# Four more buffers of weight halves between two MLPs, a lead of six units, and sums kept in PSUM

## The chip, the cores and the metric

The kernel runs on one core of a Trainium2 chip. The metric is the device time of one execution in microseconds (us), and a kernel's time is the median of its runs. An engine takes its instructions in the order of the program: TensorE (PE) multiplies, VectorE (DVE) and ScalarE (ACT) work elementwise, GpSimd (POOL) too, and SyncE (SP) issues most of the DMAs. They wait for one another by semaphores. "raw", "wh", "acc" and so on are names of buffers in the program.

## The reference, cut to what matters

Two blocks on 256 tokens of width 1024, all in fp32. The first has two layers, each a mixer and an MLP; the second is an attention block on the result and a context. The change touches the end of the first MLP, the second mixer and the second MLP:

```python
def rmsnorm(x, g):
    xf = x.astype(jnp.float32)
    y = xf * lax.rsqrt(jnp.mean(xf * xf, axis=-1, keepdims=True) + EPS)
    return (y * g.astype(jnp.float32)).astype(x.dtype)

def mixer_c(h, w_in, conv_w, conv_b, w_r, b_r, w_i, b_i, lam, w_out):
    u = h @ w_in
    gate, xr = jnp.split(u, 2, axis=-1)
    xr = causal_depthwise_conv(xr, conv_w) + conv_b
    y = rg_lru(xr, w_r, b_r, w_i, b_i, lam) * jax.nn.gelu(gate)
    return y @ w_out

def sq_relu_mlp(h, w_up, w_down):
    return jnp.square(jax.nn.relu(h @ w_up)) @ w_down

def first_block(...):
    for layer in range(DEPTH):        # DEPTH = 2
        h = rmsnorm(x, mix_norm[layer])
        y = mixer_ab(...) if layer % 2 == 0 else mixer_c(...)
        x = x + y
        x = x + sq_relu_mlp(rmsnorm(x, mlp_norm[layer]), w_up[layer], w_down[layer])
    return rmsnorm(x, final_norm)

def second_block(x, c, ctx, ...):
    shift, scale, gate = jnp.split((silu(c) @ w_mod + b_mod)[:, None, :], 3, axis=-1)
    ...
    hc = rmsnorm_2(ctx, norm_g) * (1 + scale_c) + shift_c
    ...
```

`rg_lru` makes two gates r and i from block matrices of 128 x 128, and runs the recurrence h_t = a_t h_(t-1) + b_t over the tokens.

## The kernel before, in words

Activations lie transposed, 128 features on the partitions and 256 tokens along a row, eight such tiles for the width. All large weights come as 240 units of 128 x 1024 values (512 KB), in the order in which they are used. `fetch` (L277) issues a unit's DMA on SP into one of four `raw` buffers. `prep` (L298) splits it: `wh` is the unit rounded to the matmul's format, made on ACT (L301) or DVE (L303), and `wl` what is left, made by a subtraction on DVE or POOL (L304). `POLICY` (L40) names the engines for each sort of unit, and "ag" is ACT then GpSimd, "vg" DVE then GpSimd, "av" ACT then DVE. Halves go into a ring of six slots each. `mm3` (L347) multiplies a 128 x 128 piece in three matmuls, wh·xh, wh·xl and wl·xh (L349 to L351), where xh and xl are the same two halves of the activations. A unit is 24 such matmuls of 256 columns.

`unit` (L330) hands the next unit to a matmul, and first calls `ready` until two more units than the one needed are prepared (`self.ahead`). It also runs one entry of a background list (`tick`): during MLP 0 these are the products of the second block's modulation, 40 `mdump` on DVE (L868) of 12 weight tiles `mw` of 1 MB. A scheduler then places the instructions of all engines by their order in the program and their dependencies; no order is written out by hand.

Stages: layer 0, MLP 0, layer 1, MLP 1, and the second block beginning with `b2_head`. An MLP (`mlp`, L924) takes sixteen pairs of "up" units and, two pairs later, two "down" units each, that add into four PSUM banks `acc`. Its end is `proj_tail` (L803): for each of four pairs of rows b, the last matmuls, the product `mtmp` of the bank with the row scale R2 (L820), the addition to x (L821), the scaled split `xsh`, `xsl` (L826, L832), and the square `sqt` (L840), which DVE adds to the running sums `s` (L842). POOL adds the two halves of `s` (L846).

Layer 1 (`layer1`, L968) multiplies its "xr" units by the unnormalised halves, has PE sum `s` over the partitions (L413), makes the rsqrt `rc` on POOL (L424) and spreads it by PE (L431) to R; the results are scaled by R (L1014) and go through the convolution (L1022), the gates of eight heads (`xch`, `xcl`, then L998 to L1007), the "cg" units (L1028, L1030), the scan (L1044), the split into `ysh` and `ysl` (both in a slot whose first part bears the name `xr`), and the "wo1" units. In the unit order: six xr, ri0, two xr, ri1, eight cg, eight wo1.

`b2_head` (L1083) multiplies the context's halves `hch`, `hcl` by four units into two PSUM banks `c0` and `c1`, and between them sums `s` and makes R for the second block. PSUM has eight banks, four under the tag "acc" and four under "mm", each handed out in turn.

Of the kernel before, what the change touches and what calls it, by code (L numbers as in the profile page):

```python
# [12 lines left out]
F32R = mybir.dt.float32r  # L13
AF = mybir.ActivationFunctionType
ALU = mybir.AluOpType
AX = mybir.AxisListType

T = 256
# [4 lines left out]
NEG = -1e30  # L23
CHUNK = 1
RING = 6
RAW = 4
NT = 4
MT = 28
# [216 lines left out]
class Kern:  # L245
    def __init__(self, tc, aps, names, ctx):
        self.tc, self.nc, self.a, self.names, self.ctx = tc, tc.nc, aps, names, ctx
        self.n = 0
        self.u = 0
        self.raw = None  # L250
        self.bg = []
        self.q = []
        self.cnt = {}
        self.ahead = 2

    def pool(self, name, space=None):
        return self.tc.tile_pool(name=name, bufs=1) if space is None else \
# [48 lines left out]
    def ready(self):  # L306

        i = self.u
        name = self.names[i]
        r = self.fetch(name)  # L310
        wh = self.t(self.wp, [128, 1024], "wh", F32R, bufs=RING)
        wl = self.t(self.wp, [128, 1024], "wl", F32R, bufs=RING)
        if i == 0:
            for q in range(4):
                for k in (2 * q, 2 * q + 1):
                    self.split_scaled(self.x[:, k], self.p("mix", k), self.xs[0][:, k], self.xs[1][:, k])
                if q % 2 == 0:
                    c = slice(q * 256, q * 256 + 512)
                    self.prep(r[:, c], wh[:, c], wl[:, c], "a", "v")
        elif i == 1:  # L320
            for c in (slice(0, 512), slice(512, 1024)):
                self.prep(r[:, c], wh[:, c], wl[:, c], "a", "v")
        else:
            c = POLICY.get(name, ("av",))
            c = c[self.cnt.get(name, 0) % len(c)]
            self.prep(r, wh, wl, c[0], c[1])
        self.cnt[name] = self.cnt.get(name, 0) + 1
        self.q.append((name, (wh, wl)))
# [117 lines left out]
    def run(self):  # L446
        nc, ctx = self.nc, self.ctx
        V, S, G, PE = nc.vector, nc.scalar, nc.gpsimd, nc.tensor
        self.wp = ctx.enter_context(self.pool("wp"))
        self.pad(self.wp, 384)  # L450
        self.cp = ctx.enter_context(self.pool("cp"))
        self.dp = ctx.enter_context(self.pool("dp", bass.MemoryType.DRAM))
        self.psum = ctx.enter_context(self.pool("psp", bass.MemoryType.PSUM))
        cp = self.cp
        warm = self.warm = self.t(cp, [128, 1], "warm")
        G.memset(warm, 0.0)
        S.activation(warm, warm, AF.Tanh)
        self.par = self.t(cp, [128, NPAR], "par")
        nc.sync.dma_start(self.par, self.a["par"])
        with self.pool("xp") as xp:  # L460
            self.x = self.t(xp, [128, 8, T], "x")
            self.s1 = self.t(xp, [128, 2, T], "s1")
            self.s2 = self.t(xp, [128, 2, T], "s2")
            self.ident = self.t(cp, [128, 128], "ident")
            make_identity(nc, self.ident)
            self.ones = self.t(cp, [128, 128], "ones")
            G.memset(self.ones, 1.0)
            self.mhalf = self.t(cp, [128, 4], "mhalf")
            G.memset(self.mhalf, -0.5)
            self.pad(cp, 32)  # L470
            with self.pool("l0") as lp:
                self.pad(lp, 128)
                self.layer0(lp)
            with self.pool("m0") as mp:
                self.pad(mp, 128)
                self.mod_setup(mp)
                self.mlp(mp, 0)
                self.flush()
                self.mod_finish()
            with self.pool("l1") as lp:  # L480
                self.pad(lp, 128)
                self.layer1(lp)
            with self.pool("m1") as mp:
                self.pad(mp, 128)
                self.hc = self.new_h("hc")
                self.ctx_setup(mp)
                self.mlp(mp, 1)
                self.flush()
            with self.pool("b2h") as hp:
                st = self.b2_head(hp)  # L490
        with self.pool("b2") as bp:
            self.pad(bp, 128)
            with self.pool("b2e") as ep:
                self.b2_kv(bp, ep, st)
            with self.pool("b2a") as ap:
                self.b2_attn(bp, ap, st)
            with self.pool("b2o") as op:
                self.b2_out(op, st)
        assert self.u == N_UNITS
# [303 lines left out]
    def proj_tail(self, acc, name, ins, gname, g0, xs, R2=None, mp=None, sums=(), after=None):  # L803

        nc = self.nc
        V, S, G = nc.vector, nc.scalar, nc.gpsimd
        x = self.x
        with self.tc.issue_after(after.ins) if after else nullcontext():
            ws = [self.unit(name) for _ in ins]
        n = len(ins)  # L810
        late = []
        for b in range(4):
            for i in range(n):
                self.krow(acc, ws[i], ins[i], False, i == n - 1, (2 * b, 2 * b + 1))
            xb = x[:, 2 * b:2 * b + 2]
            if R2 is None:
                V.tensor_tensor(xb, xb, self.pair(acc[b]), op=ALU.add)
            else:
                tmp = self.t(mp, [128, 2, T], "mtmp", bufs=2)
                V.tensor_tensor(tmp, self.pair(acc[b]), self.b2(R2), op=ALU.mult)  # L820
                V.tensor_tensor(xb, xb, tmp, op=ALU.add)  # L821
            ks = (2 * b, 2 * b + 1)
            g = [self.p(gname, g0 + k) for k in ks]
            if xs is not None:
                for k in ks:
                    S.activation(xs[0][:, k], x[:, k], AF.Copy, scale=g[k % 2])  # L826
            for f in late:
                f()
            late = []
            if xs is not None:  # L830
                for k in ks:
                    V.scalar_tensor_tensor(xs[1][:, k], x[:, k], g[k % 2], xs[0][:, k].bitcast(F32),  # L832
                                           op0=ALU.mult, op1=ALU.subtract)
            for i, (st, scaled) in enumerate(sums):
                q = st if b == 0 else self.t(mp, [128, 2, T], f"sqt{i}", bufs=2)
                if scaled:
                    for k in ks:
                        S.activation(q[:, k % 2], x[:, k], AF.Square, scale=self.p(scaled, k))
                else:
                    S.activation(q, xb, AF.Square)  # L840
                if b:
                    late.append(lambda st=st, q=q: V.tensor_tensor(st, st, q, op=ALU.add))  # L842
        for f in late:
            f()
        for st, _ in sums:
            G.tensor_tensor(st[:, 0], st[:, 0], st[:, 1], op=ALU.add)  # L846
# [77 lines left out]
    def mlp(self, mp, l):  # L924
        nc = self.nc
        V, S, G, PE = nc.vector, nc.scalar, nc.gpsimd, nc.tensor
        x, xs = self.x, self.xs
        acc = [self.ps("acc") for _ in range(4)]
        A = {}
        R2 = None  # L930
# [3 lines left out]
        def up(p):  # L934
            ps = first[p] if p < 2 else self.gpair(("up", "up"), xs)
            r = self.t(mp, [128, 512], "mr", bufs=2)
            a = self.t(mp, [128, 512], "ma", bufs=2)
            ah = self.t(mp, [128, 512], "mah", F32R, bufs=4)
            al = self.t(mp, [128, 512], "mal", F32R, bufs=4)
            S.activation(r, ps, AF.Relu)  # L940
            S.activation(ah, r, AF.Square)
            G.tensor_tensor(a, r, r, op=ALU.mult)  # L942
            self.lo(al, a, ah)
            A[2 * p] = (ah[:, :T], al[:, :T])
            A[2 * p + 1] = (ah[:, T:], al[:, T:])

        for p in range(16):
            up(p)
            if p == 4:
                parts = self.ssq(mp, x)  # L950
            if p == 6:
                v = self.meaneps(self.csum(parts), D)
                rv = self.t(self.cp, [128, 2], "rv")
                V.reciprocal(rv, v)
            if p == 8:
                R2 = self.spread(mp, rv, "R2")
            if p >= 2:
                for k in (2 * p - 4, 2 * p - 3):
                    self.krow(acc, self.unit("down"), A.pop(k), k == 0, False)
# [8 lines left out]
    def layer1(self, lp):  # L968
# [12 lines left out]
        gl = self.t(lp, [128, 8, T], "gl")  # L981
        parts = [self.s1[:, 0]]
        rc = []
        pss = self.gfirst("xr", xs, lambda: rc.append(self.rsq(self.meaneps(self.csum(parts), D))))
        R = self.spread(lp, rc[0], "R")

# [527 lines left out]
```

## Time and profile before

| | |
|---|---|
| Median of three runs | 834.56 us (834.39 to 838.01) |
| Profiled execution, device time | 835.34 us |
| Its span | 833.5 us |
| Mean granted clock of PE in it | 0.986 |
| PE busy | 792.4 us (95%) |
| DVE busy | 593.0 us (71%) |
| ACT busy | 457.9 us (55%) |
| POOL busy | 224.8 us (27%) |
| MLP 0 | about 115 to 298 us |
| Layer 1 | about 298 to 398 us |
| MLP 1 | about 398 to 573 us |

A row of a timeline gives start and duration in us, then engine, line and operation, what it writes and reads, how many it stands for, and in brackets how long the engine was idle before it and what ended that. The chain that ended last is 68% PE, 12% DVE and 7% DMA. Starts of matmuls of 256 columns follow one another by 0.113 us where PE is fed.

### The profile page before, as it was taken

The numbers are of one execution on the slowest core, as the hardware profiler recorded it, in microseconds if no ns is written. First come the engines' busy times: TensorE is split into PE (matmuls) and PEld (weight loads), VectorE is DVE, ScalarE is ACT, GpSimd is POOL, SyncE is SP. The second block draws the span as 40 slices with busy tenths as digits, with TensorE's granted clock in tenths as the row PEclk, the third lists the DMA queues.
The fourth block names the chain that finished last, engine by engine and source line by source line (L and its number), as shares of the span: only waits on it lengthen the run. The fifth ranks groups of instructions, "written<-read, shape, count | busy, mean of one in ns | idle before, by whom it ended". The sixth has DMA issues, their size and how long they took to land.

```text
span 833.5 us, 16173 instructions
## 1 busy us (share of the span) xinstructions
PE 792.4 (95%) x6476; PEld 759.2 (91%) x6476; DVE 593.0 (71%) x956; ACT 457.9 (55%) x722; POOL 224.8 (27%) x160
## 2 busy tenths in 40 slices
PE   7999989999899998769999999999999999999996
PEld 6997889999799988769999999999989988889996
DVE  5989669999885498997759545457633877566743
ACT  5568655444455455555756454545625587765433
POOL 4796644110111245730432111112000031320001
PEclk9999999999999999889999999999999999999998
DMA  7873357888887644336675666665234532555621
GB/s 234 280 225 128 101 184 249 270 281 309 299 255 247 184 127 152 101 102 227 210 247 172 201 187 199 187 195 179 96 122 144 177 102 102 171 168 168 201 79 51
DMA packets 41259, 152.32 MB, mean 183 GB/s; under 512 B 4576, under 2 KB 5088, under 8 KB 39008
## 3 DMA queue, kind: packets, MB, share of 16 engines
q1 hardware_dynamic: 40752, 149.19, 55.4%
q10 hardware_dynamic: 432, 2.10, 0.7%
q8 instruction: 51, 0.84, 0.4%
q14 instruction: 24, 0.20, 0.1%
HBM read 149.17 MB, written 2.10 MB: 181 GB/s over the span
## 4 chain that ended last, share of the span: by engine, by line
PE 68%; DVE 12%; DMA 7%; issue 5%; ACT 4%; POOL 3%; SPq 0%; POOLq 0%; DVEq 0%; ACTq 0%
PE mm L349 11%; PE mm L351 11%; PE mm L350 11%; PE acc L350 10%; PE acc L349 9%; PE acc L351 9%; DMA mw<-in_modw 4%; PE acc L1300 2%; DVE wl L304 2%; PE acc L1328 2%; PE mm L1337 2%; DMA raw<-in_wst 2%; ACT wh L301 1%; POOL wl L304 1%; DVE mdump L868 1%
## 5 line engine op out<-in xcount | busy, mean ns | idle before, releaser
L301 ACT ACTIVATE wh<-raw 128x1024 fp32r<-128x1024 f32 (+1 forms) x233 | 243.4, 1050 | 230.2 <-PE mm L350 87.1
L304 DVE TENSOR_TENSOR wl<-raw,wh 128x1024 fp32r<-128x1024 f32 (+1 forms) x201 | 251.1, 1256 | 128.5 <-ACT wh L301 127.2
L351 PE MATMUL mm<-xsh,wl 128*128 128x256 f32 x992 | 276.3, 279 | 2.5 <-DVE wl L304 1.5
L349 PE MATMUL mm<-xsh,wh 128*128 128x256 f32 x992 | 277.7, 280 | 0.2 <-ACT xsh L826 0.2
L350 PE MATMUL mm<-xsl,wh 128*128 128x256 f32 x992 | 276.3, 279 | 1.5 <-DVE xsl L832 1.5
L349 PEld LDWEIGHTS mm<-xsh,wh 128*128 128x128 f32 x992 | 187.6, 189 | 4.1 <-issue 3.3
L351 PEld LDWEIGHTS mm<-xsh,wl 128*128 128x128 f32 x992 | 187.3, 189 | 3.1 <-DVE wl L304 1.9
L350 PEld LDWEIGHTS mm<-xsl,wh 128*128 128x128 f32 x992 | 187.3, 189 | 2.5 <-DVE xsl L832 2.0
L351 PE MATMUL acc<-mah,wl 128*128 128x256 f32 x512 | 142.1, 278 | 3.3 <-DVE wl L304 3.3
L350 PE MATMUL acc<-mal,wh 128*128 128x256 f32 x512 | 141.7, 277 | 1.0 <-DVE mal L396 1.0
L349 PE MATMUL acc<-mah,wh 128*128 128x256 f32 x512 | 142.1, 277 | 0.0
L304 POOL TENSOR_TENSOR wl<-raw,wh 128x1024 fp32r<-128x1024 f32 x42 | 104.3, 2503 | 59.5 <-ACT wh L301 41.2
L942 POOL TENSOR_TENSOR ma<-mr 128x512 f32<-128x512 f32 x32 | 51.0, 1596 | 246.3 <-ACT mr L940 232.4
L351 PEld LDWEIGHTS acc<-mah,wl 128*128 128x128 f32 x512 | 96.2, 188 | 4.1 <-DVE wl L304 4.1
L350 PEld LDWEIGHTS acc<-mal,wh 128*128 128x128 f32 x512 | 96.3, 188 | 1.2 <-DVE mal L396 1.2
L349 PEld LDWEIGHTS acc<-mah,wh 128*128 128x128 f32 x512 | 96.1, 188 | 0.0
L868 DVE CUSTOM_DVE_ANT_0 mdump<-mw,cv 128x1024 f32<-128x1024 f32 x40 | 51.7, 1293 | 3.9 <-DMA mw<-in_modw 3.7
L350 PE MATMUL acc<-ysl,wh 128*128 128x256 f32 x128 | 37.0, 292 | 8.9 <-DVE ysl L396 8.9
L566 DVE SCALAR_TENSOR_TENSOR mm<-z,cwh,mm 128x256 f32<-128x256 f32 x106 | 44.6, 480 | 0.3
L1319 POOL TENSOR_SCALAR P<-P,st 128x512 f32<-128x512 f32 x32 | 22.3, 697 | 83.2 <-DVE st L1318 60.8
L396 DVE TENSOR_TENSOR mal<-ma,mah 128x512 fp32r<-128x512 f32 x32 | 22.8, 713 | 16.8 <-POOL ma L942 16.8
L350 PEld LDWEIGHTS acc<-ysl,wh 128*128 128x128 f32 x128 | 25.3, 198 | 9.7 <-DVE ysl L396 9.5
(346 smaller groups left out, 1335.9 us busy)
## 6 DMA issues: line engine op xcount, KB each, us to landing
raw<-in_wst SPq DMA_DIRECT2D x240, 512.0 KB, 3.7
mw<-in_modw SPq DMA_DIRECT2D x12, 1024.0 KB, 7.4
nb<-in_nab SPq DMA_DIRECT2D x16, 256.0 KB, 3.7
ab<-in_alibi ACTq DMA_DIRECT2D x1, 1536.0 KB, 9.4
x<-in_xT SPq DMA_DIRECT2D x4, 256.0 KB, 4.9
cv<-in_cvec SPq DMA_DIRECT2D x1, 1024.0 KB, 4.8
cx<-in_cT SPq DMA_DIRECT2D x1, 1024.0 KB, 4.8
xd<-x SPq DMA_DIRECT2D x1, 1024.0 KB, 4.6
```

The source lines that it names most:

```text
L301: nc.scalar.activation(wh, r, AF.Copy)
L304: (nc.vector if lo == "v" else nc.gpsimd).tensor_tensor(wl, r, wh.bitcast(F32), op=ALU.subtract)
L349: mm(out, w[0], x[0], start=start, stop=False, skip_group_check=True)
L350: mm(out, w[0], x[1], start=False, stop=False, skip_group_check=True)
L351: return mm(out, w[1], x[0], start=False, stop=stop, skip_group_check=True)
L396: self.nc.vector.tensor_tensor(l, src, h.bitcast(F32), op=ALU.subtract)
L566: return V.scalar_tensor_tensor(conv[:, j] if i == 30 else ca, zs, c, ca, op0=ALU.mult, op1=ALU.add)
L868: V.tensor_tensor_reduce(d, w, cv[:, s * 1024:(s + 1) * 1024], 0.5, 0.0, op0=ALU.mult, op1=ALU.add, accum_out=self.mod[:, s * 24 + i:s * 2 ...
L942: G.tensor_tensor(a, r, r, op=ALU.mult)
L1300: PE.matmul(sc[i], Q[tag, h][a][:, qs], K[tag, h][b], start=a + b == 0, stop=a == 1)
L1319: G.tensor_scalar(P, P, st[:, 3:4], 0.0, op0=ALU.mult, op1=ALU.add)
L1328: PE.transpose(pt[:, i * 128:(i + 1) * 128], P[:, i * 128:(i + 1) * 128], self.ident)
```

## The change

Four more slots for weight halves (pool `wx`, tags `wxh` and `wxl`) are open from MLP 0 to MLP 1. With them the ring has ten slots, from MLP 0's start until MLP 1's p = 4, where it goes back to six. From p = 10 of MLP 0 until layer 1 begins `ahead` is 6 instead of 2. In both MLPs' ends the product with R2 is written back into the PSUM bank that it reads, and the squares of b = 1 to 3 go into PSUM banks "mm" instead of SBUF. The paddings of the pools grow from 128 to 192 bytes.

```diff
+WXPAD = 192
+MPAD = 192
+EXTRA = 4
+FAR = 6
...
         r = self.fetch(name)
-        wh = self.t(self.wp, [128, 1024], "wh", F32R, bufs=RING)
-        wl = self.t(self.wp, [128, 1024], "wl", F32R, bufs=RING)
+        if self.wx is None or self.slot < RING:
+            wh = self.t(self.wp, [128, 1024], "wh", F32R, bufs=RING)
+            wl = self.t(self.wp, [128, 1024], "wl", F32R, bufs=RING)
+        else:
+            wh = self.t(self.wx, [128, 1024], "wxh", F32R, bufs=EXTRA)
+            wl = self.t(self.wx, [128, 1024], "wxl", F32R, bufs=EXTRA)
+        self.slot = (self.slot + 1) % (RING if self.wx is None else RING + EXTRA)
...
-            with self.pool("m0") as mp:
-                self.pad(mp, 128)
-                self.mod_setup(mp)
-                self.mlp(mp, 0)
...
+            with self.pool("wx") as wx:
+                self.pad(wx, WXPAD)
+                self.wx, self.slot = wx, 0
+                with self.pool("m0") as mp:
+                    self.pad(mp, MPAD)
+                    self.mod_setup(mp)
+                    self.mlp(mp, 0)
...
-                tmp = self.t(mp, [128, 2, T], "mtmp", bufs=2)
-                V.tensor_tensor(tmp, self.pair(acc[b]), self.b2(R2), op=ALU.mult)
+                tmp = self.pair(acc[b])
+                V.tensor_tensor(tmp, tmp, self.b2(R2), op=ALU.mult)
                 V.tensor_tensor(xb, xb, tmp, op=ALU.add)
...
-                q = st if b == 0 else self.t(mp, [128, 2, T], f"sqt{i}", bufs=2)
+                q = st if b == 0 else self.pair(self.ps())
...
         for p in range(16):
+            if l == 0 and p == 10:
+                self.ahead = FAR
+            if l == 1 and p == 4:
+                self.wx, self.slot = None, 0
             up(p)
...
+        self.ahead = 2
         pss = self.gfirst("xr", xs, lambda: rc.append(self.rsq(self.meaneps(self.csum(parts), D))))
```

Lines behind the first additions have other numbers after: L304 is L310, L820 is L835, L842 is L857, L846 is L861, L424 is L435, L868 is L883, L998 is L1018.

On DVE in the middle of MLP 0, before. wl_2580 is that of a "down" unit, and the rows with `mdump` are the modulation's products (each with a row that reads its sum):

```order
L304 TENSOR_TENSOR wl_2545<-raw_2542,wh_2544 128x1024
L868 ISA mdump_3163,mod_1432<-mw_3026,cv_1429 128x1024
L868 ISA mod_1432 128x1
L304 TENSOR_TENSOR wl_2580<-raw_2577,wh_2579 128x1024
L868 ISA mdump_3205,mod_1432<-mw_3203,cv_1429 128x1024
```

And after, at the same units (numbers are higher by four):

```order
L310 TENSOR_TENSOR wl_2549<-raw_2546,wh_2548 128x1024
L883 ISA mdump_2780,mod_1436<-mw_2746,cv_1433 128x1024
L883 ISA mod_1436 128x1
L883 ISA mdump_2820,mod_1436<-mw_2746,cv_1433 128x1024
L883 ISA mod_1436 128x1
L310 TENSOR_TENSOR wl_2584<-raw_2581,wh_2583 128x1024
```

The same `wl` has fewer products ahead of it: the one in front of wl_2580 is the 32nd of the forty, the two in front of wl_2584 are the 22nd and the 23rd.

On POOL at the end of MLP 0, before. wl_3562, wl_3734 and wl_3782 are of xr units, wl_3881 is of ri0, `s` is the sum behind the MLP and `rc` the rsqrt that layer 1 waits for:

```order
L942 TENSOR_TENSOR ma_3466<-mr_3465 128x512
L304 TENSOR_TENSOR wl_3562<-raw_3559,wh_3561 128x1024
L304 TENSOR_TENSOR wl_3734<-raw_3731,wh_3733 128x1024
L304 TENSOR_TENSOR wl_3782<-raw_3779,wh_3781 128x1024
L846 TENSOR_TENSOR s_5_76<-s_5_76 128x256
L976 MEMSET xr_3715 128x8x3
L304 TENSOR_TENSOR wl_3881<-raw_3878,wh_3880 128x1024
L424 TENSOR_TENSOR rc_3820<-var_3818,mhalf_85 128x2
L304 TENSOR_TENSOR wl_3951<-raw_3948,wh_3950 128x1024
```

And after:

```order
L310 TENSOR_TENSOR wl_3538<-raw_3535,wh_3537 128x1024
L310 TENSOR_TENSOR wl_3578<-raw_3575,wh_3577 128x1024
L957 TENSOR_TENSOR ma_3494<-mr_3493 128x512
L310 TENSOR_TENSOR wxl_3590<-raw_3587,wxh_3589 128x1024
L310 TENSOR_TENSOR wxl_3881<-raw_3878,wxh_3880 128x1024
L995 MEMSET xr_3739 128x8x3
L310 TENSOR_TENSOR wl_3951<-raw_3948,wh_3950 128x1024
L861 TENSOR_TENSOR s_5_76<-s_5_76 128x256
L310 TENSOR_TENSOR wl_4026<-raw_4023,wh_4025 128x1024
L310 TENSOR_TENSOR wl_4056<-raw_4053,wh_4055 128x1024
L435 TENSOR_TENSOR rc_3820<-var_3818,mhalf_85 128x2
```

The units stand earlier against `s`: wl_3951 moved from behind `rc` to ahead of `s`. Two `wl` now stand between `s` and `rc` where one stood, and nine are left behind `rc` where twelve were.

On DVE at the end of MLP 1, before; `acc_4721` and `acc_4722` are the last two banks of the MLP:

```order
L820 TENSOR_TENSOR mtmp_6891<-acc_4722,R_870_5779 128x512
L842 TENSOR_TENSOR s_5_76<-s_5_76,sqt_1014_6862 128x512
L821 TENSOR_TENSOR x_75<-x_75,mtmp_6891 128x512
L842 TENSOR_TENSOR s_6_77<-s_6_77,sqt_1015_6864 128x512
L304 TENSOR_TENSOR wl_6920<-raw_6917,wh_6919 128x1024
```

And after:

```order
L835 TENSOR_TENSOR acc_4722<-acc_4722,R_867_5779 128x512
L857 TENSOR_TENSOR s_5_76<-s_5_76,mm_6859 128x512
L836 TENSOR_TENSOR x_75<-x_75,acc_4722 128x512
L857 TENSOR_TENSOR s_6_77<-s_6_77,mm_6861 128x512
L310 TENSOR_TENSOR wl_6917<-raw_6914,wh_6916 128x1024
```

The order is the same. The squares are now `mm` tiles: six of them take the four banks in turn, and the seventh tile of the tag, `c0`, gets the bank of the third, mm_6859.

## Rows read from the trace of the kernel before

**Rows 1.** The page, busy us of each engine, share, instructions:

```profile
PE 792.4 (95%) x6476; PEld 759.2 (91%) x6476; DVE 593.0 (71%) x956; ACT 457.9 (55%) x722; POOL 224.8 (27%) x160
```

**Rows 2.** Busy us in stretches A:B: length, then engines, granted clock, DMA share, GB/s:

```profile
180.00:230.00 50.00, 45.36 (x382) 44.36 (x383) 46.22 (x64) 21.44 (x25) 5.27 (x4) 1.00 0.84 291
230.00:298.00 68.00, 68.00 (x602) 68.00 (x601) 44.16 (x53) 36.22 (x44) 12.08 (x7) 1.00 0.68 215
...
330.00:398.00 68.00, 55.88 (x435) 54.68 (x436) 62.53 (x77) 38.40 (x62) 22.70 (x8) 0.90 0.44 140
```

**Rows 3.** Waits of PE, 180 to 230 us: us in total, times, longest:

```profile
PE acc L351 <- DVE wl L304: 3.3, 4, 1.4
PE mm L351 <- DVE wl L304: 1.5, 2, 1.3
```

**Rows 4.** Waits of PE, 284 to 390 us:

```profile
PE acc L350 <- DVE ysl L396: 6.2, 1, 6.2
PE acc L350 <- DVE xcl L396: 5.0, 4, 2.1
PE acc L349 <- ACT xr L388: 1.6, 1, 1.6
...
PE mm L351 <- POOL wl L304: 0.9, 1, 0.9
PE mm L431 <- POOL rc L424: 0.8, 1, 0.8
```

**Rows 5.** Timeline of DVE in MLP 0: start, us, operation, idle before:

```profile
218.32 1.23 DVE L868 CUSTOM_DVE_ANT_0 mdump<-mw,cv 128x1024 f32<-128x1024 f32 x1 [1.22 <-DMA mw<-in_modw]
...
219.47 1.22 DVE L304 TENSOR_TENSOR wl<-raw,wh 128x1024 fp32r<-128x1024 f32 x1
```

**Rows 6.** Timeline of DVE from MLP 0's end to the scans of layer 1:

```profile
299.04 0.68 DVE L820 TENSOR_TENSOR mtmp<-acc,R 128x512 f32<-128x512 f32 x1
...
301.98 2.88 DVE L821 TENSOR_TENSOR x<-x,mtmp 128x512 f32<-128x512 f32 x1
...
364.47 5.51 DVE L1044 TENSOR_TENSOR_SCAN xc<-r,ig 128x256 f32<-128x256 f32 x2
...
370.49 1.26 DVE L1044 TENSOR_TENSOR_SCAN xc<-r,ig 128x256 f32<-128x256 f32 x2
```

**Rows 7.** Timeline of POOL in the same stretch:

```profile
298.61 2.77 POOL L304 TENSOR_TENSOR wl<-raw,wh 128x1024 fp32r<-128x1024 f32 x1 [7.39 <-ACT wh L301]
301.81 2.50 POOL L304 TENSOR_TENSOR wl<-raw,wh 128x1024 fp32r<-128x1024 f32 x1 [0.44 <-ACT wh L301]
308.07 0.73 POOL L846 TENSOR_TENSOR s<-s 128x256 f32<-128x256 f32 x1 [3.76 <-DVE s L842]
...
309.48 2.40 POOL L304 TENSOR_TENSOR wl<-raw,wh 128x1024 fp32r<-128x1024 f32 x1
311.83 1.98 POOL L424 TENSOR_TENSOR rc<-var,mhalf 128x2 f32<-128x2 f32 x1
...
363.84 5.60 POOL L304 TENSOR_TENSOR wl<-raw,wh 128x1024 fp32r<-128x1024 f32 x2 [5.86 <-ACT wh L301]
```

**Rows 8.** PE alone in three stretches: length, busy (matmuls), granted clock, DMA:

```profile
343.90:349.00 5.10, 5.09 (x24) 0.51 0.41 112
...
372.30:376.00 3.70, 3.62 (x17) 0.50 0.03 8
376.00:390.00 14.00, 14.00 (x124) 0.99 0.79 245
```

**Rows 9.** The page's DMA issues: KB each, us from issue to landing:

```profile
raw<-in_wst SPq DMA_DIRECT2D x240, 512.0 KB, 3.7
```

**Rows 10.** Timelines of DVE and PE at MLP 1's end:

```profile
573.22 0.68 DVE L820 TENSOR_TENSOR mtmp<-acc,R 128x512 f32<-128x512 f32 x1
573.82 0.68 DVE L842 TENSOR_TENSOR s<-s,sqt 128x512 f32<-128x512 f32 x1
...
572.79 0.28 PE L349 MATMUL mm<-hch,wh 128*128 128x256 f32 x1
```

More of the change, by code (lines that the diff above doesn't have):

```diff
@@ L254, in __init__ @@
         self.ahead = 2
+        self.wx = None
+        self.slot = 0
     def pool(self, name, space=None):
@@ L473, in run @@
                 self.layer0(lp)
-            with self.pool("m0") as mp:
-                self.pad(mp, 128)
-                self.mod_setup(mp)
-                self.mlp(mp, 0)
[L478 to L488, printed above, removed]
+            with self.pool("wx") as wx:
[5 more added lines that the diff above has]
+                    self.mlp(mp, 0)
+                    self.flush()
+                    self.mod_finish()
+                with self.pool("l1") as lp:
+                    self.pad(lp, MPAD)
+                    self.layer1(lp)
+                with self.pool("m1") as mp:
+                    self.pad(mp, MPAD)
+                    self.hc = self.new_h("hc")
+                    self.ctx_setup(mp)
+                    self.mlp(mp, 1)
+                    self.flush()
+                assert self.wx is None
             with self.pool("b2h") as hp:
```

## The prediction

> **What bounds the kernel now.** I read the page first: TensorE (PE) is busy for 95% of the span, VectorE (DVE) for 71% [rows 1]. A share that high says that only PE's idle time can be won, so the next view was busy time by stretch. PE is full from 230 to 298 us, and short of work in two stretches: 45.4 of 50 us at MLP 0's middle, and 55.9 of 68 us (at 0.90 of full clock) in the second part of layer 1; DVE is at 92% in both [rows 2]. The waits of PE then say for what. At MLP 0's middle every wait is for `wl`, the low half of a weight unit made on DVE: 3.3 + 1.5 = 4.8 us [rows 3]. In layer 1 the largest is 6.2 us for `ysl`, the low half of layer 1's first scan outputs [rows 4]. So the kernel is bound by PE, and in these two places by DVE, which works in order.
>
> DVE is late for two different reasons. At MLP 0 it has the `mdump` products of the modulation in front of the `wl` that PE wants: at 218.32 it stands 1.22 us for `mw`, then multiplies for 1.23, and only then makes the next `wl` [rows 5]. In layer 1 it stands still while GpSimd (POOL) makes its own `wl`: two scans begun at 364.47 end at 369.98, where a pair beginning at 370.49 takes 1.26 us [rows 6], and POOL's two `wl` run from 363.84 to 369.44 [rows 7].
>
> **The change, part by part.**
>
> *Lead at MLP 0's end.* Four more slots and a lead of six units let `ready()` run four units further from p = 10. Nothing is removed: each unit still costs one DMA, one cast on ACT (or DVE) and one subtraction on DVE or POOL. What moves is the order: in the rows of DVE the same `wl` now has 8 to 10 fewer `mdump` in front of it. Nine of those at some 1.2 us [rows 5] are 11 us, more than the 4.8 us that PE waits for. So I take the whole 4.8 us as gone. Bounds: 2 us if the first of those waits (0.4 and 0.5 us long, before the lead has built up) and half of the others stay, 7 us if small spacing losses beside them go too. The displaced products still fit: DVE has 24 us free between 230 and 298 (44.2 busy of 68) [rows 2]. Four extra casts on ACT cost nothing, since PE is not waiting for ACT there [rows 3].
>
> *From MLP 0 to layer 1.* Here the order on POOL changes. Before, one `wl` stands between the sum `s` and the rsqrt `rc`; after, two. One takes 2.40 us, and PE waits 0.8 us for `rc` already [rows 4, 7]. Against that, `s` comes earlier: in before, DVE's add of the last rows (L821, both operands in SBUF) takes 2.88 us because POOL's `wl` from 301.81 to 304.31 blocks it, while L820, with one operand in PSUM, took 0.68 beside another `wl` of POOL [rows 6, 7]. With the product now in PSUM, the add becomes like L820: 2.2 us earlier, of which I count 1.3 for `s` since the squares on ACT still stand between. Net: `rc` and the first matmul behind it 2.40 - 1.3 = 1.1 us later; bounds -1 (the second `wl` is done before `s` comes) and +2 us.
>
> The Trainium skill (SBUF — State Buffer, "Who interferes with whom") says that a DVE instruction with two SBUF inputs contends with a GpSimd instruction that reads SBUF, and one with at most one SBUF input does not, outside its two-port modes. L820 and L821 agree with it. By the rule the adds of the sums (L842) are freed as well; if it didn't hold for operands in PSUM written by ACT, this part would be 2.4 instead of 1.1 us.
>
> *Layer 1.* Before, eight of POOL's twelve `wl` behind `rc` fall between 334 and 370 us, in the DVE chain that ends at `ysl`. With four units more of lead only four (of cg6, cg7 and the first two of wo1) are left for that stretch. A blocked operation is one of 0.4 to 0.7 us that lasts until POOL is done, so each of POOL's `wl` costs DVE about 2 us (5.51 - 1.26 = 4.25 for two [rows 6]). Four fewer are 8 us, and `ysl` is ready about 7 us earlier than at 372 us. PE's wait of 6.2 us is then gone, the 1.6 us for `xr`, the high half in front of it, too [rows 4], and with the standstill the slow clock: after it PE ran 17 matmuls in 3.70 us at 0.50 of the clock where they take 17 x 14.00/124 = 1.9 at 0.99 [rows 8], 1.8 us. Together 6.2 + 1.6 + 1.8 = 9.6 us. Bounds: 0, if another wait takes their place, and 10.2 with the spacing between the waits.
>
> What could take their place is ACT: two casts of wo1's units now stand right in front of the tanh of head 4, and their loads are issued only once POOL has read the slots of cg6 and cg7; a load lands in 3.7 us [rows 9]. ACT stood idle before that tanh, so most is hidden, but heads 6 and 7 get their `xch` later. PE waits 5.0 us for `xcl` in four places [rows 4]: two of them should shrink with fewer POOL blocks, one or two grow with ACT. I leave the 5.0 us as they are and add 0.7 us; bounds -4 and +4. The 0.9 us for POOL's `wl` [rows 4] goes with the lead. Rest of layer 1: 0.7 - 0.9 = -0.2 us.
>
> *Sums in PSUM at MLP 1's end.* The six squares now rotate through four PSUM banks, and the bank of `c0`, the first context product after the MLP, comes free only when DVE has added the square that stands behind the fourth L820. Before, PE went on at 572.79 without a gap, and that addition ended at 573.82 + 0.68 = 574.50 [rows 10]. So PE now waits some 1.7 us; I take +1.7. Bounds 0 (if ACT and DVE are earlier by as much) and +4 (a clock that falls as after the wait at 343.91, which cost 24 matmuls 5.10 - 24 x 14.00/124 = 2.4 us [rows 8]).
>
> *Operands in PSUM.* L820 reads PSUM and takes 0.68 us, L842 reads SBUF alone and takes 0.68 [rows 10]; nothing is gained or lost on a free DVE. The other paddings shift addresses; the trace shows no cost of an address, and I take 0, bounds -1 and +1.
>
> **Sum.** -4.8 + 1.1 - 9.6 - 0.2 + 1.7 = -11.8 us. The profiled execution took 835.34 us in all (833.5 span), which gives 823.5; that execution is 0.8 us above the median of the runs shown, 834.56, so the same sum on the median gives 822.8. I say 823.
>
> **Rivals.**
>
> 1. *Only MLP 0's gain.* ACT, not DVE, becomes the one that layer 1's end waits for: it stands behind loads of wo1 in front of the tanh of head 4 and of head 6, twice up to 3.7 us [rows 9], the scans begin 7 us later than forecast, and PE's wait at `ysl` returns. For it: in the order these casts do move in front of the tanh. Against: ACT was idle there, and PE's matmuls for those heads come no sooner. Time: 834.56 - 4.8 + 1.1 + 1.7 - 0.2, less some of the clock, 831 to 832; with half of the wait back 827.
>
> 2. *The lead does not grow.* There are still four `raw` buffers, so a unit is loaded only when the fourth before it has been split. If loads beside the 1 MB `mw` transfers hold the preparation back, the new slots stay empty, no wait goes, and the waits at `rc` and `c0` remain: 834.56 + 1.1 + 1.7 = 837. Against: PE waits for `wl` behind DVE, never for a `raw` load, in both stretches [rows 3, 4].
>
> 3. *The slower side: products waiting for `mw` with `wl` queued behind them.* Ten products are pushed to 235 to 260 us, and their `mw` loads behind more `raw` loads on the same queue. DVE is in order: each of some five late `mw` would hold it as at 218.32 (1.22 us [rows 5]) or for twice that, 6 to 12 us in all. The lead of six units is 6 x 24 matmuls x 0.113 us [rows 8] = 16 us of PE's work; only if the waits use up this and the free 24 us of DVE does PE pay. Then MLP 0's 4.8 us stay, layer 1 begins without a lead and its 9.6 us stay, and about 4 us of new waits come on top: 834.56 + 1.1 + 1.7 + 4 = 841. Against: the transfers have room between 230 and 298 us, where PE is full [rows 2].
>
> **How the numbers follow.** Forecast (DVE's chain shorter in both places) 0.66, 818 to 828; rival 1 0.14; rival 2 0.10; rival 3 0.06; a larger gain, where waits for `xcl` go too, 0.04 at 816 to 818. A measurement of this kernel can tell 0.5%, 4.2 us: faster is below 830.4, slower above 838.7. Faster: 0.66 + 0.04 + 0.09 of rival 1 = 0.79; same: 0.05 of rival 1, rival 2, less 0.01 that lands above, 0.14; slower 0.07. Range 815.5 to 831: it takes in rival 1 with its half returns and leaves out rivals 2 and 3.
>
> **What would show it.** Right: no PE wait for `wl` between 180 and 298 us; DVE's free time there moved from after 250 us to before; L821 at MLP 0's end at 0.7 us; the wait at `rc` at 1.5 to 2.5 us; at most four of POOL's `wl` between the gates and the scans; the wait at `ysl` under 1 us and no slow clock behind it; a wait of 1.5 to 2 us of the first matmul into `c0`, released by the add of a square. Wrong: waits for `xcl` that sum to more than 8 us, ACT idle on `raw` in layer 1, a wait at `ysl` over 3 us, or a PE wait for `wl` after 230 us.

## The result, and the profile after

The changed kernel is faster, by about half of what was forecast: median 830.69 us over ten runs (826.13 to 835.59), before 837.90 over ten on the same chip; the ratio of the means is 0.9927, 95% interval 0.9903 to 0.9952, so 6.1 us less (7.2 by the medians) where 11.8 were forecast. (Before's median lies above the 834.56 of the three runs shown ahead; only ratios of runs on one chip are used below.) The profiled execution took 829.35 us (835.34 before), 6.0 us less, and shows where. The table sets the first matmuls of the stages side by side, from the timelines of PE, and the length of each stage (the first row runs from PE's first matmul, the last to its last):

| stage, from its first matmul to the next one's | before, us | after, us | difference | forecast |
|---|---|---|---|---|
| ahead of MLP 0 (not touched) | 110.0 | 109.1 | -0.9 | 0 |
| MLP 0 to the sum of `s` | 194.1 | 188.3 | -5.8 | -4.8 |
| sum of `s` to the spread of `rc` | 5.0 | 7.2 | +2.2 | +1.1 |
| spread to the first gate | 8.8 | 10.6 | +1.8 | 0 |
| first gate to the first wo1 matmul | 43.1 | 43.0 | -0.1 | -1.8 |
| first wo1 matmul to the first on `ysl` | 6.6 | 0.3 | -6.3 | -6.2 |
| that to the first into `c0` | 200.4 | 204.1 | +3.7 | -0.1 |
| from `c0` to the end | 253.7 | 253.1 | -0.6 | 0 |

(The forecast's -1.6 us for `xr`, -0.9 and +0.7 stand in the fifth row, its -1.8 for the clock and +1.7 for `c0` in the seventh.) Each column is one execution. E3 below, the same order of instructions run once more, differs from after by 1.2 us in the second row, 0.3 in the third and 1.5 in the seventh; E5 to E7, whose edits lie behind MLP 0, have 189.6 to 190.1 us in the second row and 6.5 to 6.7 in the third. So up to 1.8 us in the second row, 0.7 in the third and 1.5 in the seventh can be noise; the fourth row is 10.6 us in all of these. The two large gains came where they were forecast. Four losses eat half of them. PE's waits of after from MLP 0's end to MLP 1's start, to be held against [rows 4] (us in total, times, longest); between 180 and 282 us there is none, where [rows 3] had 4.8 us:

```profile
PE acc L361 <- DVE xcl L407: 7.7, 4, 5.1
PE mm L361 <- DVE xsl L847: 3.4, 4, 1.5
PE mm L442 <- POOL rc L435: 3.0, 1, 3.0
PE mm L424 <- POOL s L861: 0.6, 1, 0.6
```

No row for `ysl` or the high half `xr` is left. But `rc` has grown from 0.8 to 3.0 us, `xcl` from 5.0 to 7.7. Of the 3.4 us for `xsl`, 1.5 lie at MLP 0's end, where before had as much (first row below); the rest is new, at MLP 1's start (the other two rows: after, 380 to 400 us, where before has no wait):

```profile
PE mm L350 <- DVE xsl L832: 1.5, 2, 1.2
...
PE mm L361 <- DVE xsl L847: 1.9, 3, 0.9
PE mm L360 <- ACT xsh L841: 0.2, 1, 0.2
```

Each such wait also delays the matmuls around it: by their starts, the four gaps at MLP 1's start cost 3.0 us. POOL of after, to be held against [rows 7]:

```profile
301.16 1.10 POOL L861 TENSOR_TENSOR s<-s 128x256 f32<-128x256 f32 x1 [4.08 <-DVE s L857]
302.23 5.61 POOL L310 TENSOR_TENSOR wl<-raw,wh 128x1024 fp32r<-128x1024 f32 x2
307.80 1.68 POOL L435 TENSOR_TENSOR rc<-var,mhalf 128x2 f32<-128x2 f32 x1
...
332.17 5.48 POOL L310 TENSOR_TENSOR wxl<-raw,wxh 128x1024 fp32r<-128x1024 f32 x2 [6.07 <-PE mm L362]
337.61 5.29 POOL L310 TENSOR_TENSOR wl<-raw,wh 128x1024 fp32r<-128x1024 f32 x2
```

Two `wl`, 5.61 us in all, stand between `s` and `rc`. The last four, of cg6, cg7 and wo1, run in a row from 332.17 to 342.90. DVE in the same places (the first three rows, like the first of [rows 6], are MLP 0's end; the next four lie beside POOL's four; the last four are MLP 1's start):

```profile
292.73 4.64 DVE L847 SCALAR_TENSOR_TENSOR xsl<-x,par,xsh 128x256 fp32r<-128x256 f32 x2
297.29 0.67 DVE L836 TENSOR_TENSOR x<-x,acc 128x512 f32<-128x512 f32 x1
...
303.04 2.58 DVE L309 CAST wh<-raw 128x1024 fp32r<-128x1024 f32 x1
...
332.83 2.62 DVE L1026 TENSOR_TENSOR xc<-r 128x512 f32<-128x512 f32 x1 [0.19 <-ACT r L1023]
...
335.76 2.44 DVE L1027 SCALAR_TENSOR_TENSOR th<-xc,th 128x512 f32<-128x512 f32 x1
...
338.51 2.17 DVE L407 TENSOR_TENSOR xcl<-xc,xch 128x256 fp32r<-128x256 f32 x1
...
341.00 2.19 DVE L407 TENSOR_TENSOR xcl<-xc,xch 128x256 fp32r<-128x256 f32 x1
...
384.75 1.23 DVE L310 TENSOR_TENSOR wl<-raw,wh 128x1024 fp32r<-128x1024 f32 x1 [0.82 <-ACT wh L307]
385.89 0.88 DVE L847 SCALAR_TENSOR_TENSOR xsl<-x,par,xsh 128x256 fp32r<-128x256 f32 x2
...
387.27 1.22 DVE L310 TENSOR_TENSOR wl<-raw,wh 128x1024 fp32r<-128x1024 f32 x1
388.41 0.88 DVE L847 SCALAR_TENSOR_TENSOR xsl<-x,par,xsh 128x256 fp32r<-128x256 f32 x2
```

Each of POOL's four holds one DVE operation of 0.4 to 0.7 us until it is done, four in a row, and the last two are the `xcl` that PE waits for. At 303.04 a cast, which reads one operand, is held in the same way: 2.58 us beside POOL's first `wl` behind `s`, where one at 291.35, with POOL idle, took 0.69. At MLP 1's start a `wl` of 1.2 us now stands in front of each `xsl`. PE's own timeline shows the largest wait, and at MLP 1's end the one at `c0` that was forecast at 1.7:

```profile
340.74 0.58 PE L361 MATMUL acc<-xcl,wh 128*128 128x256 f32 x1 [5.10 <-DVE xcl L407]
...
567.61 0.38 PE L360 MATMUL mm<-hch,wh 128*128 128x256 f32 x1 [1.59 <-DVE s L857]
```

And PE alone (length, busy, matmuls, granted clock) behind the wait for `rc` and around that for `xcl`:

```profile
309.50:314.00 4.50, 4.47 (x25) 0.62 0.53 161
340.00:348.00 8.00, 6.41 (x28) 0.50 0.50 163
```

Behind the wait of 3 us PE is given 0.62 of its clock in that stretch: 16 starts, from 310.43 to 313.82, lie about 0.21 instead of 0.113 us apart (1.6 us), which is most of the +1.8 in the fourth line of the table. Before, at the same place, the clock was full (first row below). The length of this wait alone does not decide it: in E2 below, where it is 2.60 us, the clock stays full (second row), and in E7, where it is 2.39 us, it falls (third row). What else does is open.

```profile
313.80:318.30 4.50, 4.44 (x38) 1.00 0.70 243
311.80:316.30 4.50, 4.50 (x39) 1.00 0.48 161
312.40:316.90 4.50, 4.50 (x25) 0.62 0.55 179
```

### The profile page after: what moved, and what is told of

Read it like the earlier page. It is cut to its first block, busy times and chain, and to the rows that moved or that the text cites. A ratio compares the mean times of both kernels' runs of the same rounds, so it can differ in the third digit from the quotient of the medians.

```text
span 827.5 us, 16152 instructions
## 1 busy us (share of the span) xinstructions
PE 790.3 (96%) x6476; PEld 757.8 (92%) x6476; DVE 589.2 (71%) x956; ACT 457.4 (55%) x722; POOL 220.6 (27%) x160
## 4 chain that ended last, share of the span: by engine, by line
PE 74%; DVE 11%; ACT 5%; DMA 3%; issue 3%; POOL 2%; SPq 0%; POOLq 0%; DVEq 0%; ACTq 0%
PE mm L360 13%; PE mm L361 13%; PE mm L362 12%; PE acc L361 10%; PE acc L360 9%; PE acc L362 9%; DMA raw<-in_wst 3%; PE acc L1320 2%; PE acc L1348 2%; PE mm L1357 2%; DVE wl L310 2%; ACT wh L307 1%; DVE ysl L407 1%; POOL wl L310 1%; PE mm L442 1%
## 5 line engine op out<-in xcount | busy, mean ns | idle before, releaser
L307 ACT ACTIVATE wh<-raw 128x1024 fp32r<-128x1024 f32 (+1 forms) x198 | 207.1, 1049 | 185.6 <-PE mm L361 77.3
L310 DVE TENSOR_TENSOR wl<-raw,wh 128x1024 fp32r<-128x1024 f32 (+1 forms) x167 | 208.8, 1257 | 109.5 <-ACT wh L307 109.4
L361 PE MATMUL mm<-xsl,wh 128*128 128x256 f32 x824 | 229.7, 279 | 1.5 <-DVE xsl L847 1.5
L360 PE MATMUL mm<-xsh,wh 128*128 128x256 f32 x824 | 231.0, 280 | 0.0
L362 PE MATMUL mm<-xsh,wl 128*128 128x256 f32 x824 | 229.6, 279 | 0.0
L310 POOL TENSOR_TENSOR wl<-raw,wh 128x1024 fp32r<-128x1024 f32 x36 | 87.9, 2463 | 27.9 <-ACT wh L307 27.2
L307 ACT ACTIVATE wxh<-raw 128x1024 fp32r<-128x1024 f32 x35 | 36.6, 1056 | 34.7 <-DMA raw<-in_wst 27.0
L883 DVE CUSTOM_DVE_ANT_0 mdump<-mw,cv 128x1024 f32<-128x1024 f32 x40 | 51.0, 1274 | 3.4 <-DMA mw<-in_modw 3.1
L310 DVE TENSOR_TENSOR wxl<-raw,wxh 128x1024 fp32r<-128x1024 f32 x34 | 43.7, 1305 | 9.4 <-ACT wxh L307 9.4
L361 PE MATMUL mm<-xsl,wxh 128*128 128x256 f32 x168 | 47.5, 283 | 1.9 <-DVE xsl L847 1.9
L360 PE MATMUL mm<-xsh,wxh 128*128 128x256 f32 x168 | 47.6, 284 | 0.2 <-ACT xsh L841 0.2
L362 PE MATMUL mm<-xsh,wxl 128*128 128x256 f32 x168 | 47.2, 281 | 0.0
```

What stands on the lines that cost most here:

```text
L307: nc.scalar.activation(wh, r, AF.Copy)
L310: (nc.vector if lo == "v" else nc.gpsimd).tensor_tensor(wl, r, wh.bitcast(F32), op=ALU.subtract)
L360: mm(out, w[0], x[0], start=start, stop=False, skip_group_check=True)
L361: mm(out, w[0], x[1], start=False, stop=False, skip_group_check=True)
L362: return mm(out, w[1], x[0], start=False, stop=stop, skip_group_check=True)
L883: V.tensor_tensor_reduce(d, w, cv[:, s * 1024:(s + 1) * 1024], 0.5, 0.0, op0=ALU.mult, op1=ALU.add, accum_out=self.mod[:, s * 24 + i:s * 2 ...
```

## The experiments

**One part alone.** The first three take the change apart.

E1, before with the sums in PSUM alone:

```diff
-                tmp = self.t(mp, [128, 2, T], "mtmp", bufs=2)
+                tmp = self.pair(acc[b])
...
-                q = st if b == 0 else self.t(mp, [128, 2, T], f"sqt{i}", bufs=2)
+                q = st if b == 0 else self.pair(self.ps())
```

> The kernel before with the sums in PSUM alone (product back into the bank, squares in mm banks), no new slots, lead 2. Theory A (the sums cost about as much as they give): the add of the last rows at MLP 0's end falls from 2.9 to 0.7 us, rc comes about 1 us earlier; the first product into c0 waits 1.5 to 2 us for the add of a square. Total +0 to +2 us, ratio 1.000 to 1.002; the wait at ysl stays near 6 us and those for wl in MLP 0 near 5 us. Rival (freeing DVE from POOL at MLP 0's end carries into layer 1): ysl's wait falls by more than 2 us and the total is 3 us below before.

Ratio 1.0025 (1.0002 to 1.0048): this part costs 0 to 4 us by itself. The wait at `c0` is there (1.59 us), the ones for `ysl` (6.2) and `wl` stay. The rows of DVE and then POOL at MLP 0's end show why nothing was won there; the last row is DVE in the kernel before:

```profile
300.64 2.93 DVE L832 SCALAR_TENSOR_TENSOR xsl<-x,par,xsh 128x256 fp32r<-128x256 f32 x2
...
304.69 0.67 DVE L821 TENSOR_TENSOR x<-x,acc 128x512 f32<-128x512 f32 x1
305.29 2.60 DVE L304 TENSOR_TENSOR wl<-raw,wh 128x1024 fp32r<-128x1024 f32 x1
...
300.28 2.62 POOL L304 TENSOR_TENSOR wl<-raw,wh 128x1024 fp32r<-128x1024 f32 x1 [7.75 <-PE acc L350]
304.41 2.40 POOL L304 TENSOR_TENSOR wl<-raw,wh 128x1024 fp32r<-128x1024 f32 x1
...
299.64 2.42 DVE L832 SCALAR_TENSOR_TENSOR xsl<-x,par,xsh 128x256 fp32r<-128x256 f32 x2
```

The addition is free of POOL, as forecast, but the next operation with both operands in SBUF stands still in its place; before, too, each of POOL's two `wl` held one operation, `xsl` and then the addition. Theory A held but for one part: `rc` does not come earlier (PE still waits 0.8 us for it), and so the 1.3 us that the prediction took off for `s` did not hold either.

E2, the changed kernel with the sums back in SBUF (E1's edit the other way).

> The changed kernel with the sums in SBUF as before; the new slots and the lead stay. Theory A: no wait at c0, so MLP 1's end is 1.7 us better than in the changed kernel; at MLP 0's end the add blocked by POOL returns (2 us), but POOL's order still has two wl between s and rc, so the wait at rc stays about 3 us or grows to 4 to 5. Total 5 to 8 us below before, ratio 0.990 to 0.994. Rival (the sums in PSUM are what moved rc and the tail): the wait at rc falls under 1.5 us and the total is more than 9 us below before.

Ratio 0.9942 (0.9922 to 0.9962), PE still waits 2.6 us for `rc` and up to 5.1 for `xcl`, and not at `c0`. The slots alone carry the whole gain; theory A held. The 1.7 us of `c0` are less than such ratios tell apart.

E3, the changed kernel with FAR = 2.

> The changed kernel with a lead of two units (FAR = 2) instead of six; the four slots stay. Theory A (the scheduler fills free slots whatever the lead says, and the slots do it all): the same waits as in the changed kernel to 0.3 us each (rc 3.0, xcl 5.1, xsl at MLP 1's start 2.7 in all, c0 1.6, none for wl at MLP 0's middle), ratio 0.990 to 0.995; what differs from the changed kernel is the noise of a kernel run twice. Rival (the lead of six makes MLP 0's gain): wl waits of 3 to 5 us return between 180 and 230 us, ratio 0.997 to 1.000.

Ratio 0.9944 (0.9922 to 0.9967), and no wait for `wl` between 180 and 282 us. With names' numbers left out, the order of all five engines is the same as with FAR = 6: the scheduler prepares units as slots come free, and the lead of six changes nothing here. So this is the changed kernel run twice.

**The losses one by one.** E4 issues POOL's `wl` behind `rc`:

```diff
+        with self.tc.issue_after(self.hold.ins) if self.hold and lo == "g" else nullcontext():
...
+        self.hold = self.lastr    # the pow that makes rc; None again behind ri(1)
```

> The changed kernel, but POOL's wl of the units that are prepared behind rc in the program are issued only after rc, so that none stands between the sum s and rc. Theory A (POOL's order alone makes the late rc): the wait at rc falls from 3.0 to 0.3 us or less, and the half-speed matmuls behind it (18 at 0.21 instead of 0.11 us, 1.8 us) go too; R is 2.5 to 4.5 us earlier. How much of it stays is open: with POOL's wl later the wait for xcl of head 4 (5.1 us) could grow by the same. Total against the changed kernel -1 to -4 us, ratio to before 0.988 to 0.991. Rival (rc waits for the sum, or DVE's var, not for POOL's wl): the wait stays above 2 us and the time is that of the changed kernel.

The wait at `rc` is gone, and with it the slow clock: from the sum to the spread 4.0 us instead of 7.2. On POOL:

```profile
301.33 0.73 POOL L863 TENSOR_TENSOR s<-s 128x256 f32<-128x256 f32 x1 [3.81 <-DVE s L859]
304.65 1.62 POOL L437 TENSOR_TENSOR rc<-var,mhalf 128x2 f32<-128x2 f32 x1 [2.58 <-DVE var L432]
```

Yet the ratio is 0.9957 (0.9934 to 0.9981), no better. From the spread to the first gate it takes 10.7 us as in the changed kernel: eight more matmuls of the xr units fall behind the spread, and the first gate waits 1.2 us for `xch` of ACT. The waits behind it, and one of POOL's late `wl` with the three scans of DVE beside it:

```profile
PE acc L363 <- DVE xcl L409: 7.8, 5, 3.0
PE acc L363 <- DVE ysl L409: 3.4, 1, 3.4
...
359.75 2.40 POOL L312 TENSOR_TENSOR wl<-raw,wh 128x1024 fp32r<-128x1024 f32 x1 [5.87 <-ACT wh L308]
...
359.80 4.06 DVE L1068 TENSOR_TENSOR_SCAN xc<-r,ig 128x256 f32<-128x256 f32 x3
```

`ysl`'s wait is back with 3.4 us: the same POOL work, done later, holds DVE later (the three scans take 4.06 us, where two take 1.26 in [rows 6]). Counted from MLP 0's start, PE reaches its first matmul on `ysl` 1.7 us earlier than in the changed kernel, and from there to `c0` it takes 208.0 instead of 204.1 us. Theory A was right on the cause of the wait and wrong on its worth.

E5 goes back to six slots before wo1 (`self.wx, self.slot = None, 0` moved there from MLP 1).

> The changed kernel, but the ring goes back from ten to six slots before wo1 instead of in MLP 1. Theory A (with ten slots free the scheduler puts a wl between each addition to x and the low half xsl behind it, 1.2 us each): at MLP 1's start DVE's order is that of before, and PE's four waits for xsl and xsh there (3.0 us) fall under 0.5 us. MLP 1's start 2.5 to 3 us earlier, ratio to before 0.989 to 0.992. Rival (DVE is simply full there, whatever stands first): the waits for xsl become waits for wl or mal of about the same sum, and the time is the changed kernel's.

Ratio 0.9866 (0.9835 to 0.9897). DVE's order at MLP 1's start is that of before, and PE has no wait between 380 and 400 us; from the first matmul on `ysl` to `c0` it takes 200.4 us instead of 204.1. Theory A held, by a little more than its size.

E6 frees `c0`'s bank:

```diff
-                q = st if b == 0 else self.pair(self.ps())
+                q = st if b == 0 else self.pair(self.ps()) if b < 3 or len(sums) == 1 else self.t(mp, [128, 2, T], f"sqt{i}")
```

> The changed kernel with MLP 1's last two squares in SBUF, so that the bank of c0 is one that came free two pairs of rows earlier. Theory A: the wait of 1.6 us of the first product into c0 goes; the wait for the last sum (0.2 us) comes back; MLP 1's end is 1.4 to 1.8 us earlier, everything before it as in the changed kernel. Ratio 0.990 to 0.993. Rival (c0 waits for DVE anyway): the wait stays over 1 us under another name.

The wait went, that for the last sum (0.2 us) came back, and the ratio is 0.9935 (0.9905 to 0.9965): the mechanism is shown in the profile, its 1.6 us are too small for the ratio.

E7 takes the last four `wl` from POOL, and two casts from DVE to ACT with them:

```diff
-... cg=("vg",))
+... cg=("vg",) * 6 + ("av",) * 2)
-POLICY["wo1"] = ("ag",) * 2 + ("av",) * 6
+POLICY["wo1"] = ("av",) * 8
```

> The changed kernel, but the wl of the last two cg units and of the first two wo1 units are made on DVE (cast on ACT), not on POOL: the four that stand in a row beside the xcl of heads 4 and 5. DVE gets 4 x 1.2 us and loses two casts of 0.7. Theory A (POOL's blocking makes the wait of 5.1 us for xcl of head 4): that wait falls to 2 us or less, and with it the half-speed matmuls behind it (2 us); wo1 begins 3 to 5 us earlier than in the changed kernel, ratio 0.988 to 0.991 as far as MLP 1's start lets it through. Rival (DVE's own load bounds the stretch): the wait moves to ysl or wl with 3 us or more, wo1's second unit begins within 1 us of the changed kernel's.

Ratio 0.9829 (0.9790 to 0.9867), some 8 us better than the changed kernel, more than either theory gave. The waits:

```profile
PE acc L361 <- DVE xcl L407: 1.8, 2, 1.4
PE acc L361 <- DVE ysl L407: 1.6, 1, 1.6
```

From the first gate to the first wo1 matmul it takes 34.8 us instead of 43.0; of these 8.2 us, 2.0 are lost again in front of `ysl`. DVE has four `wl` more of 1.2 us and two casts less of 0.7, and is done sooner.

**Together.** E8 has E4 to E7 in one, E11 the same without E4's.

> The changed kernel with all four: rc ahead of POOL's wl, no late wl on POOL, ring back before wo1, c0's bank free. Theory A (four separate losses: 2 to 4 us at rc with the clock, 4 at xcl, 3 at xsl, 1.6 at c0, of which rc's was shown to be lost again behind POOL in layer 1): 7 to 10 us below the changed kernel, ratio 0.980 to 0.985. Rival (layer 1 is bound by DVE from its first results on, so that rc and xcl give only one gain): 3 to 6 us, ratio 0.986 to 0.989.

> The version with all four less the one at rc: POOL's order between s and rc as in the changed kernel, the late wl on DVE, ring back before wo1, c0's bank free. Theory A (rc's gain is passed on only in part, 1 to 2 us): 1 to 2 us slower than the version with all four, ratio 0.979 to 0.983. Rival (all of it is lost again behind POOL in layer 1): the same time as with all four, wo1's second unit at the same distance from MLP 0's start to 0.5 us.

E8 0.9779 (0.9741 to 0.9816), E11 0.9800 (0.9739 to 0.9860): E8 gains somewhat more than theory A gave (its 0.980 lies within the interval), E11 about as much; whether `rc`'s gain is passed on these ratios leave open. In the profiles, counted from MLP 0's start, E8 has the spread of `rc` 6.5 us ahead of E11, and at the first matmul on `ysl` 2.1 us of that are left.

E9 goes on from E7: ri, cg and wo1 are all "av", with E5's and E6's edits. E10 is the kernel before with that policy alone, no new slot:

```diff
-... ri=("vg",), cg=("vg",))
+... ri=("av",), cg=("av",))
-POLICY["wo1"] = ("ag",) * 2 + ("av",) * 6
+POLICY["wo1"] = ("av",) * 8
```

> The changed kernel with ring back before wo1, c0's bank free, and every unit of ri, cg and wo1 cast on ACT and subtracted on DVE, so that POOL makes no wl behind rc at all. DVE gains nine wl of 1.2 us in place of casts of 0.7 and of being blocked about 2 us by each of POOL's. Theory A (POOL's wl cost DVE more in this stretch than they save): the waits for xcl, 8 us in the changed kernel, fall under 4 us, rc's under 0.5 us; 8 to 12 us below the changed kernel, ratio to before 0.978 to 0.984. Rival (DVE's sum of work bounds layer 1): waits for wl of cg or wo1 and for ysl of 5 us or more appear, ratio 0.986 to 0.992.

> The kernel before (six slots, lead two, sums in SBUF) with the same units of ri, cg and wo1 taken from POOL. Theory A (layer 1's late ysl in the kernel before was POOL's blocking, the new slots helped only by moving those wl away): ysl's wait of 6.2 us falls under 2 us without any new slot, MLP 0's waits for wl (4.8 us) stay; 5 to 9 us below before, ratio 0.989 to 0.994. Rival (the slots themselves, as a lead in layer 1, are what removed the wait): ysl's wait stays over 4 us, ratio 0.997 or more.

E9 0.9700 (0.9659 to 0.9740), and PE waits in it for neither `xcl` nor `rc`; E10 0.9823 (0.9786 to 0.9860). Theory A held in both, by more than its size. E10 is the telling one: without any slot it gains some 15 us, more than twice the change. Its waits from 282 to 400 us, of which `ysl` had 6.2 and `xcl` 5.0 before, and those of 180 to 230 us, where the slots are missing:

```profile
PE acc L349 <- ACT xr L388: 4.1, 1, 4.1
PE mm L350 <- DVE xsl L832: 1.5, 2, 1.2
PE acc L350 <- DVE ysl L396: 0.6, 1, 0.6
```

```profile
PE acc L351 <- DVE wl L304: 2.6, 2, 2.3
PE mm L351 <- DVE wl L304: 1.2, 1, 1.2
```

The groups of DVE from 305 to 372 us show the mechanism (count, busy us, mean ns of one, idle before); L1006 of before, of after (L1026), of E9 (L1024) and of E10 (L1006 again) is the same operation on SBUF operands:

```profile
L1006 DVE TENSOR_TENSOR xc<-r 128x512 f32<-128x512 f32 x4 | 6.8, 1698 | 0.0
```

```profile
L1026 DVE TENSOR_TENSOR xc<-r 128x512 f32<-128x512 f32 x4 | 4.7, 1169 | 0.2 <-ACT r L1023 0.2
```

```profile
L1024 DVE TENSOR_TENSOR xc<-r 128x512 f32<-128x512 f32 x4 | 2.8, 692 | 0.2
```

```profile
L1006 DVE TENSOR_TENSOR xc<-r 128x512 f32<-128x512 f32 x4 | 2.7, 682 | 0.0
```

1698 and 1169 ns with twelve and nine `wl` of POOL behind `rc`, 692 with none in E9 and 682 with one, at 314.76 us, in E10. E9 and E10 also move ten casts from DVE to ACT. That alone does not relieve DVE: ten casts of 0.7 us are 7 us, and the twelve `wl` of 1.2 us that E10 gives it in their place are 14.6. A run that moves the casts alone was not made. E12 takes the four xr units of MLP 0's end from POOL as well (`xr=("av",)`).

> The version without POOL's wl behind rc (ring back, c0's bank free), and the four xr units that POOL still makes around MLP 0's end are made on DVE too. Theory A (POOL's wl block DVE at MLP 0's end as in layer 1): the waits there for xsl and s (1.4 and 1.2 us) fall under 0.5 us each, 1 to 3 us below the version with POOL's four, ratio to before 0.966 to 0.970. Rival (DVE is the one that is full at MLP 0's end, four more wl of 1.2 us stand in front of the tail): the waits for xsl, mal or wl there grow to 4 us or more, 1 to 4 us above it, ratio 0.971 to 0.975.

Ratio 0.9704 (0.9665 to 0.9743): the wait for `xsl` there is gone, that for `s` stays at 1.0 us, and the time is E9's within the intervals. Inconclusive. E9 and E12 beat both kernels: 3.0% below before.

## Why the prediction was wrong

The two large gains were forecast rightly; what failed are the terms for what takes the place of the waits that went. That 830.69 us lies just inside the range of 815.5 to 831 and near rival 1's 831 to 832 is luck: the range reaches so far for a wait at `ysl` that comes back, and none came back.

- *Lead at MLP 0's end*: right in effect (-5.8 us for -4.8, no wait for `wl` left), wrong in its cause. E3 shows that the lead of six does nothing; ten slots do it. The 1.0 us between the two is less than one execution tells.
- *From MLP 0 to layer 1*: the step that `rc` comes 1.1 us later failed. It came 2.2 us later (2.96 us of wait; 1.5 to 2.2 us with E3 and E5 to E7), since the 1.3 us taken off for an earlier `s` did not exist: the addition was freed, and `xsl` and `wl` were held in its place (E1), so that PE's wait for `s` went from 0.3 to 0.6 us. And behind the wait for `rc` came 1.6 us of slow clock, which the prediction left out here, though it counted such a loss behind `ysl` and as a bound at `c0`. E4 shows POOL's two `wl` as the cause of the wait.
- *Layer 1*: the waits for `ysl` and `xr` went as forecast, and four of POOL's `wl` fewer did it. What failed is "what could take their place is ACT": it was POOL again. The four that were left ran in a row beside the `xcl` of heads 4 and 5, and PE's wait there grew from 2.1 to 5.1 us (E7 removes it). The waits for `xcl` sum to 7.7 us, just under the 8 that the prediction named as a sign of being wrong. Rival 1 had the stretch right, and the engine (ACT) and the wait (`ysl`) wrong.
- *MLP 1's start*: no term at all. I followed the new slots in MLP 0 and layer 1 and not where they let DVE's `wl` move in front of `xsl`: 3.0 us by the starts of the matmuls, 2.1 of them waits (E5 removes them).
- *Sums in PSUM*: the wait at `c0` was 1.6 us, forecast 1.7; this term was right.
- Rivals 2 and 3 did not happen: preparation moved four units ahead, and no `mw` held PE.

By size, measured less forecast from the table: -1.0 at MLP 0, +1.1 at `rc`, +1.8 behind it, +1.7 up to wo1, -0.1 at `ysl` and +3.8 up to `c0` are 7.3 us; the two stages at the ends, which the change hardly touches, moved by -1.5, and 5.8 remain.

The rule of the Trainium skill (SBUF — State Buffer, "Who interferes with whom") agrees with these rows: E1's addition, with one operand in PSUM, ran at 0.67 us beside POOL, and of the operations with two in SBUF each of POOL's `wl` held one until it was done. The cast that was held for 2.58 us reads one operand only; the rule as the prediction gives it leaves room for that in its two-port modes, but no run here shows in which mode a cast runs. E10 shows how much the holding was worth here.

## What to carry to other kernels

When a second engine's help holds up the one that is late, price the help by what it blocks: a POOL instruction of 2.4 us held DVE about 2 us to save it 1.2, and taking the help away gained more than the buffers. A buffer that frees a scheduler moves work everywhere it is open: look at each short operation that the critical engine waits for, and close the ring before it where something now stands in front. Time won ahead of a stretch that another engine bounds is passed on only in part: of 6.5 us at `rc`, 2.1 were left at `ysl` (E8 against E11).

## What the runs showed of the hardware

The starts of matmuls are not always 0.113 us apart at full granted clock. PE of before, and of E1, in the same 40 us of MLP 1, with no wait in either:

```profile
376.00:416.00 40.00, 40.00 (x353) 1.00 0.68 222
```

```profile
376.00:416.00 40.00, 40.00 (x341) 1.00 0.65 213
```

In E1 they are 0.118 us apart from 376 to 436 us (mean of the timeline), 4% more, or some 2 us in that stretch; E6 shows the same, other profiles shorter ones. What makes them was not tried. The ten runs of one kernel spread over 1%, and this may be part of it.
